# Homes for two loaded weight tiles of a Strassen product: the hi and lo rings instead of buffers of v and x

## The chip, the core and the metric

The kernel runs on one core of a Trainium2 chip. The metric is the device time of one execution in microseconds (us); smaller is better. A second number, the span, is the time from the first to the last instruction of a profiled execution.

## What is computed

Two layers of a decoder trunk on 256 tokens of width 1024, all in float32. Each layer is a half-step feed-forward block (FFN), a mixer, and a second FFN, each with a residual and a layer norm:

```python
def _swiglu(x, w1, w3, w2):
    return (jax.nn.silu(x @ w1) * (x @ w3)) @ w2
...
    for l in range(DEPTH):
        h = _swiglu(x, ffn_w1[l, 0], ffn_w3[l, 0], ffn_w2[l, 0])
        x = _layernorm(ALPHA * x + 0.5 * h, ln_g[l, 0], ln_b[l, 0])
        h = _mixer(x, l, w_in[l], ...)
        x = _layernorm(ALPHA * x + h, ln_g[l, 1], ln_b[l, 1])
        h = _swiglu(x, ffn_w1[l, 1], ffn_w3[l, 1], ffn_w2[l, 1])
        x = _layernorm(ALPHA * x + 0.5 * h, ln_g[l, 2], ln_b[l, 2])
```

`w1` and `w3` are 1024 x 2816, `w2` is 2816 x 1024. There are so four FFNs and four multiplications by `w2`. They are called stage one to four here, in the order in which they run. The mixer plays no part in what follows.

## The kernel before

**Split multiplication.** A float32 matrix is multiplied as the sum of a rounded part (hi) and the rest (lo): ACT copies the weights to the rounded type (hi), DVE subtracts hi from the weights (lo), and PE makes three matmuls for each piece: hi by hi, lo by hi, hi by lo. Every weight that is used goes this way: SP loads 1 MB (128 x 2048) into a buffer of the `raw` pool (`fetch`, line 159), then `stream` (176) or `pieces` (359) splits it in two halves of 128 x 1024, each into one buffer of the `hi` pool (`whi` in the profile) and one of the `lo` pool (`wlo`). `raw` has 4 buffers, `hi` and `lo` have 8 each (line 46); a hi or lo buffer holds 4 KB a partition and is free again when PE has read it.

**The FFN.** In the order of PE, which is written out by hand: products by `w1` and `w3` in column blocks, with one more block done by Strassen's scheme in between (`seven`, line 837: seven block products in place of eight; sums of weight blocks are made on DVE). Then the last `w13a` columns (`gemm_a2`, 285): four halves of hi are multiplied in one pass (line 295, L295 in the profile), then their four halves of lo in a second pass (L302). So w13a holds four lo buffers into the second pass. The next stretch is `w2`.

**The w2 stage** (`gemm_seven`, 377). The first eight row blocks of `w2` (1024 rows, 1024 columns) are split in four blocks w11, w12, w21, w22 of 1 MB each and multiplied by Strassen's scheme; each product is 12 matmuls (`product`, 369; L373). Between the products, one unit (`between`, 412; L402, 12 matmuls) of the remaining rows is done, from chunks of 1 MB that `rest` streams in (two units a chunk). The program's order is:

- load w11 as r1 and split it (p1); load w12 as **r2**; r1 += r2 (`plus`, 353, on DVE, L356)
- product p1; unit; load and split w21, product; add w22 to r2 with accumulating DMAs on POOL's queue (`gather`, 347); load w22 as **r3**
- unit; split r1 (now w11 + w12), product, `fold` the result into the residual (line 602, L605 `xtok` in the profile)
- unit; split r3, product; unit; r1 += r3, split, product, fold; add w21 to r1 with accumulating DMAs
- unit; split r2, product, fold; two units; split r1, product, fold; then the second column half of the remaining rows

r2 and r3 are the two tiles that are loaded to be summed up. **Before**, their homes are called `spare` (lines 924 and 925): r2's halves lie in the two `val` buffers of the `act` pool, which in the mixer hold the values v of the attention and in the FFN the `planes` tiles of blocks n = 0 and n = 2; r3 lies in one buffer of the `xs` pool, whose two buffers hold the split x that w1 and w3 are multiplied by, until the L302 pass has read it. The same scheme in the w13 block (`seven`, lines 859 and 864) has its r2 and r3 in two buffers of `hi` and two of `lo`.

**What sets the order.** PE's order is the program's. On ACT and DVE the splits and the `plus` of the FFN from its second column block on are chained in the program's order (`inline`, 150, and `behind`, 155); other instructions are put between them. SP's, POOL's and the rest of ACT's and DVE's order is made when the program is built, by the framework: the instruction with the lowest number of `step` (109) that has its inputs and a buffer goes first, and a buffer goes to whoever asks for it once it is free. On the chip each queue then runs strictly in that order and waits on semaphores.

Of the kernel before, what the change touches and what calls it, by code (L numbers as in the profile page):

```python
# [11 lines left out]
F32 = mybir.dt.float32  # L12
# [8 lines left out]
P = 128  # L21
D = 1024
# [15 lines left out]
HC = CH // 2  # L38
# [16 lines left out]
def trunk(ctx, tc, x, xT, w13a, w13b, w2, wb, wqk, wu, wg, wgr, wbr, wbrr, wo, gateb, gatebr, sgug, sgub, sguwT, sgubias, lam, diffg,  # L55
# [7 lines left out]
    hi_pool = ctx.enter_context(tc.tile_pool(name="hi", bufs=HL))  # L63
    lo_pool = ctx.enter_context(tc.tile_pool(name="lo", bufs=HL))
    xs = ctx.enter_context(tc.tile_pool(name="xs", bufs=2))
    act = ctx.enter_context(tc.tile_pool(name="act", bufs=26))
# [7 lines left out]
    def name(s):  # L74
        serial[0] += 1
        return f"{s}_{serial[0]}"
# [32 lines left out]
    def step():  # L109
        chunk[0] += 1  # L110
        tc.cur_priority = chunk[0] * STEP
# [43 lines left out]
    def behind(ins):  # L155

        return tc.issue_after(ins) if ins is not None else nullcontext()

    def fetch(src, width=CH, raw=None):

        step()
        if raw is None:
            raw = raw_pool.tile([P, CH], F32, tag="raw", name=name("raw"))
        for g in gate:
            g[0] -= 1
        while len(gate) > 1 and gate[1][0] < 0:
            gate.pop(0)
        with behind(gate[0][1] if gate and gate[0][0] < 0 else None):
            if isinstance(raw, list):
                for j, v in enumerate(raw):  # L170
                    loaded[0] = nc.sync.dma_start(v, src[:, j * HC : (j + 1) * HC]).ins
            else:
                loaded[0] = nc.sync.dma_start(raw[:, :width], src).ins
        return raw
# [149 lines left out]
    def gemm_b(src, kts, xh, xl, done, tail=4, last=()):  # L324
# [13 lines left out]
        for t in range(NT):  # L338
            for ps, o, n in blocks[t]:
                for k, piece in held:  # L340
                    rows_b(ps, t, k, piece, xh, xl, kts, o, n)
                done(t, ps[:, :n], o, n)

    def halved(v):
        return v if isinstance(v, list) else [v[:, o : o + HC] for o in range(0, CH, HC)]

# [6 lines left out]
    def plus(raw, more):  # L353
        for v, m in zip(halved(raw), halved(more)):
            with behind(line[1]):
                inline(V, V.tensor_tensor(out=v, in0=v, in1=m, op=ALU.add).ins)  # L356
        return raw
# [16 lines left out]
                          skip_group_check=True)  # L374
            beat(0.25)

    def gemm_seven(src, xh, xl, sums, spare, ln, done):

# [31 lines left out]
        def between():  # L412
            k, piece = next(first)
            for t in range(NT):
                rows(t, 0, k, piece)

        r1 = fetch(w11)
        p1 = pieces(r1)
        r2 = fetch(w12, raw=spare[0])
        plus(r1, r2)  # L420
        product(bx, a11, p1, True, False)
        ln.fold(0, 0, bx, ALU.add, True)
        between()
        product(q[0][0], a12, pieces(fetch(w21)), False, False)
        gather(r2, w22)
        r3 = fetch(w22, raw=spare[1])
        between()
        product(bz, sums[0], pieces(r1), True, False)
        ln.fold(1, 1, bz, ALU.add, True)
# [313 lines left out]
    def ffn(l, f, i, norm, last=False):  # L743
        xh, xl = parts(both)
# [11 lines left out]
        hh, hl = hv(h_hi), hv(h_lo)  # L756
# [42 lines left out]
        held, sums = {}, []  # L799
# [37 lines left out]
        def seven(src, x_sums):  # L837
# [18 lines left out]
            yield  # L856
            if norm:
                crossed(fetch(w21))
            r2 = fetch(w12, raw=[hi_pool.tile([P, HC], F32, tag="hi", name=name("r2")) for _ in range(2)])
            if norm:  # L860
                yield
            product(bz, x_sums[0], pieces(plus(r1, r2)), True, False)
            A.activation(v1, bz, AF.Copy)
            r3 = fetch(w22, raw=[lo_pool.tile([P, HC], F32, tag="lo", name=name("r3")) for _ in range(2)])
            yield
            product(bx, x_sums[1], pieces(plus(r1, r3)), False, False)
            A.activation(v0, bx, AF.Copy)
# [50 lines left out]
        for j in range(FA, FT - 4, 2):  # L918
            for m, z in gemm_a2([w13a[l, f, j - FA + m] for m in range(2)], both, lambda m: t512("silu")):
# [1 line left out]
                silu[0] = A.activation(s, s, AF.Silu).ins  # L921
                V.tensor_tensor(out=s, in0=s, in1=z[:, T:], op=ALU.mult)
                split(*(v[-1][:, (j - FA + m) * T : (j - FA + m + 1) * T] for v in (h_hi, h_lo)), s)
        spare = [[act.tile([P, D], F32, tag="val", name=name("spare"), bufs=2) for _ in range(2)],
                 xs.tile([P, 4, 512], F32, tag="x", name=name("spare")).rearrange("p k c -> p (k c)")]
        ln = Norm(l, i, 2.0 * ALPHA, 4.0 * EPS, s[:, :1], last)

        def done(t, p, c, n):
# [1 line left out]
            if c + n == D:  # L930
                ln.finish(t, 1.9)

        gemm_seven([w2[l, f, c] for c in range(2)], hh, hl, sums, spare, ln, done)
        return ln.close()

    def mixer(l, i, norm):
# [388 lines left out]
```

## Time and profile before

| what | value |
|---|---|
| median of 3 runs | 1200.97 us (1199.14 to 1205.47) |
| profiled execution | 1208.93 us |
| its span | 1206.9 us |
| mean granted TensorE clock | 0.997 |
| HBM read | 249.10 MB, 207 GB/s over the span |
| the chain that ended last | PE 87%, DMA 5%, DVE 5% |
| of it, loads into `spare` (r2, r3) | 3.5% |

A row of a timeline is: start in us, duration in us, engine, line of the kernel, operation, tile written <- tiles read, shapes, count (xN: N instructions of one kind merged), and in brackets the idle time of the engine ahead of it and what ended that. SPq rows are DMAs that SP issues; their duration is that of the issue, not of the transfer. A row of the waits view is: who waited for whom, us in all, times, longest. A row of windows is: the window, its length, then for PE, PEld, DVE, ACT and POOL the busy time and the count of instructions, then the granted clock, the share of the DMA engines and GB/s. A row of a tile view is: line, engine, operation, tiles, count, then the least, median and greatest duration in ns and the first and last start in us. A row of DMA issues ends with the size of one and the median us from issue to landing. Buffer numbers are left out of names: `spare` is r2 and r3 of the w2 stages, `raw<-in_w` are loads of w2.

### The profile page before, as it was taken

The page shows a single profiled execution, that of the slowest core. Times are in us where ns is not written, and L with a number is a line of the kernel's source. Part 1 is how long each engine was busy: PE and PEld are TensorE (multiplying, and loading weights), DVE is VectorE, ACT ScalarE, POOL GpSimd, SP SyncE. Part 2 cuts the span into 40 slices and gives each one's busy share as a digit, 9 for nine tenths or more (in the row PEclk, how much of TensorE's full clock was granted, in tenths as well). Part 3 has the DMA queues.
Part 4 walks back from the last instruction along what each step waited for, and adds up shares of the span by engine and source line. Part 5 has one row for each costly group of instructions (what it writes and reads, how often), then busy time and mean ns, then how long its engine had stood idle before and what let it go on. Part 6 is the DMA issues. An engine that isn't in the chain of part 4 may idle for free.

```text
span 1206.9 us, 16650 instructions
## 1 busy us (share of the span) xinstructions
PE 1186.2 (98%) x5771; PEld 995.5 (82%) x5771; DVE 1012.0 (84%) x1558; ACT 824.1 (68%) x1418; POOL 296.6 (25%) x356
## 2 busy tenths in 40 slices
PE   9999899999999999999999999999999999999898
PEld 7888688888888888887888888788888888888777
DVE  6889878877778989879899878988966989989685
ACT  6688557559964676885567875676788556679650
POOL 1111301137520210071020070004564012103400
PEclk9999999999999999999999999999999999999999
DMA  9869784767855758697768698586675764886870
GB/s 348 282 194 280 241 292 169 254 201 216 263 190 189 242 175 272 195 284 219 268 206 266 179 277 275 202 288 227 217 211 192 250 192 153 281 257 221 210 241 36
DMA packets 129220, 276.14 MB, mean 229 GB/s; under 512 B 89024, under 2 KB 90096, under 8 KB 104560
## 3 DMA queue, kind: packets, MB, share of 16 engines
q1 hardware_dynamic: 121392, 248.80, 61.6%
q0 software_dynamic: 7312, 25.76, 9.2%
q8 instruction: 45, 0.74, 0.2%
q10 hardware_dynamic: 432, 0.52, 0.2%
q14 instruction: 39, 0.32, 0.1%
HBM read 249.10 MB, written 1.05 MB: 207 GB/s over the span
## 4 chain that ended last, share of the span: by engine, by line
PE 87%; DMA 5%; DVE 5%; ACT 1%; issue 1%; SPq 0%; ACTq 0%; DVEq 0%
PE bank L283 45%; PE bank L295 13%; PE sbank L373 9%; PE bank L302 7%; PE bank L402 5%; DMA spare<-in_w 3%; PE sbank L402 3%; PE bank L512 2%; DVE wlo L249 1%; DMA raw<-in_w 1%; DVE wlo L197 1%; PE sbank L984 1%; DVE raw L356 1%; PE sbank L1040 1%; PE sbank L1158 1%
## 5 line engine op out<-in xcount | busy, mean ns | idle before, releaser
L197 DVE TENSOR_TENSOR wlo<-raw,whi 128x1024 fp32r<-128x1024 f32 (+1 forms) x374 | 414.0, 1134 | 50.1 <-ACT whi L195 35.1
L195 ACT ACTIVATE whi<-raw 128x1024 fp32r<-128x1024 f32 (+1 forms) x378 | 351.5, 958 | 119.2 <-PE bank L283 43.8
L283 PE MATMUL bank<-whi,x 128*128 128x512 f32 x1224 | 386.5, 390 | 0.0
L283 PEld LDWEIGHTS bank<-whi,x 128*128 128x128 f32 x1224 | 229.9, 188 | 47.3
L283 PE MATMUL bank<-wlo,x 128*128 128x512 f32 x612 | 238.5, 390 | 0.0
L295 PE MATMUL bank<-x,whi 128*128 128x512 f32 x640 | 153.3, 392 | 0.0
L295 PEld LDWEIGHTS bank<-x,whi 128*128 128x128 f32 x640 | 118.3, 188 | 23.7
L247 ACT ACTIVATE whi<-raw 128x1024 fp32r<-128x1024 f32 (+1 forms) x96 | 92.6, 982 | 65.4 <-DVE raw L356 31.2
L283 PEld LDWEIGHTS bank<-wlo,x 128*128 128x128 f32 x612 | 115.0, 188 | 23.4
L249 DVE TENSOR_TENSOR wlo<-raw,whi 128x1024 fp32r<-128x1024 f32 (+1 forms) x96 | 110.7, 1166 | 20.1 <-ACT whi L247 19.8
L229 POOL COPY seven<-seven 128x512 uint16<-128x512 uint16 x16 | 64.7, 4102 | 108.7 <-ACT whi L195 82.1
L302 PEld LDWEIGHTS bank<-x,wlo 128*128 128x128 f32 x640 | 81.4, 192 | 2.9
L302 PE MATMUL bank<-x,wlo 128*128 128x256 f32 x640 | 82.6, 284 | 0.0
L402 PE MATMUL bank<-whi,hhi 128*128 128x512 f32 (+1 forms) x182 | 68.8, 378 | 2.9 <-DVE silu L305 2.9
L402 PE MATMUL bank<-wlo,hhi 128*128 128x512 f32 (+1 forms) x182 | 68.1, 374 | 0.0
L402 PE MATMUL bank<-whi,hlo 128*128 128x512 f32 (+1 forms) x182 | 68.0, 374 | 0.0
L960 POOL TENSOR_TENSOR swap<-swap,sin_t 128x512 f32<-128x512 f32 x16 | 26.4, 1649 | 103.3 <-DVE wlo L197 46.1
L719 POOL COPY nvia<-ntwo 128x256 uint16<-128x256 uint16 x20 | 9.9, 544 | 153.3 <-DMA ntwo<-nvia 109.0
L303 ACT ACTIVATE r<-bank 128x256 f32<-128x256 f32 x96 | 33.9, 371 | 13.1 <-PE bank L302 13.0
L402 PEld LDWEIGHTS bank<-whi,hhi 128*128 128x128 f32 x182 | 34.4, 189 | 9.7 <-DVE silu L305 3.8
L373 PE MATMUL sbank<-whi,sum 128*128 128x512 f32 x96 | 33.9, 416 | 8.4 <-DVE xtok L605 8.4
L373 PE MATMUL sbank<-whi,xhs 128*128 128x512 f32 x128 | 42.0, 390 | 0.0
(286 smaller groups left out, 2164.7 us busy)
## 6 DMA issues: line engine op xcount, KB each, us to landing
raw<-in_w13b SPq DMA_DIRECT2D x68, 1024.0 KB, 5.4
raw<-in_w SPq DMA_DIRECT2D x32, 1024.0 KB, 7.1
raw<-in_wb SPq DMA_DIRECT2D x16, 1024.0 KB, 5.3
raw<-in_wqk SPq DMA_DIRECT2D x16, 1024.0 KB, 6.3
r<-in_w13b SPq DMA_DIRECT2D x16, 512.0 KB, 5.9
raw<-in_w13a SPq DMA_DIRECT2D x8, 1024.0 KB, 4.8
raw<-in_wgr SPq DMA_DIRECT2D x8, 1024.0 KB, 5.2
raw<-in_wg SPq DMA_DIRECT2D x8, 1024.0 KB, 5.4
```

The lines of the kernel that those rows point to most:

```text
L195: inline(A, A.activation(h, r, AF.Copy).ins)
L197: low = eng.tensor_tensor(out=w, in0=r, in1=h.bitcast(F32), op=ALU.subtract).ins
L229: eng.tensor_copy(out=o, in_=i)
L247: a = A.activation(hi, src, AF.Copy).ins
L249: return a, eng.tensor_tensor(out=lo, in0=src, in1=hi.bitcast(F32), op=ALU.subtract).ins
L283: PE.matmul(ps, xx, w, start=start and n == 0, stop=stop and n == 2)
L295: PE.matmul(b[-1], hi[:, k * P : (k + 1) * P], xc(k), start=k == 0, stop=False)
L302: PE.matmul(b[n][:, :T], lo[:, k * P : (k + 1) * P], xc(k)[:, :T], start=False, stop=k == KT - 1)
L303: emptied[0] = A.activation(r[:, s], b[n][:, T:], AF.Copy, scale=scale).ins
L373: PE.matmul(ps, x[o](k), y, start=start and k == n == 0, stop=stop and k == 3 and n == 2, skip_group_check=True)
L402: PE.matmul(q[c][t][:, :n] if o == 0 else more[:, :n], x(k, t), y, start=k == 8 and m == 0 and (c, t) != (1, 0), stop=k == FT - 1 and m == ...
L960: turned_by[0] = G.tensor_tensor(out=s3, in0=s3, in1=s, op=ALU.mult).ins
```

## The change

`gemm_seven` no longer gets `spare`. r2 lies in two buffers of the `hi` pool and r3 in two of the `lo` pool, asked for at the place of their loads; r3 is so loaded by two DMAs of 512 KB instead of one of 1 MB. The new helper `homes` makes such a pair; the w13 block uses it too, for the same buffers as before.

```diff
+    def homes(pool, tag):
+        return [pool.tile([P, HC], F32, tag=tag, name=name("home")) for _ in range(2)]
+
...
-    def gemm_seven(src, xh, xl, sums, spare, ln, done):
+    def gemm_seven(src, xh, xl, sums, ln, done):
...
         r1 = fetch(w11)
         p1 = pieces(r1)
-        r2 = fetch(w12, raw=spare[0])
+        r2 = fetch(w12, raw=homes(hi_pool, "hi"))
         plus(r1, r2)
         product(bx, a11, p1, True, False)
         ln.fold(0, 0, bx, ALU.add, True)
         between()
         product(q[0][0], a12, pieces(fetch(w21)), False, False)
         gather(r2, w22)
-        r3 = fetch(w22, raw=spare[1])
+        r3 = fetch(w22, raw=homes(lo_pool, "lo"))
...
-            r2 = fetch(w12, raw=[hi_pool.tile([P, HC], F32, tag="hi", name=name("r2")) for _ in range(2)])
+            r2 = fetch(w12, raw=homes(hi_pool, "hi"))
...
-            r3 = fetch(w22, raw=[lo_pool.tile([P, HC], F32, tag="lo", name=name("r3")) for _ in range(2)])
+            r3 = fetch(w22, raw=homes(lo_pool, "lo"))
...
-        spare = [[act.tile([P, D], F32, tag="val", name=name("spare"), bufs=2) for _ in range(2)],
-                 xs.tile([P, 4, 512], F32, tag="x", name=name("spare")).rearrange("p k c -> p (k c)")]
...
-        gemm_seven([w2[l, f, c] for c in range(2)], hh, hl, sums, spare, ln, done)
+        gemm_seven([w2[l, f, c] for c in range(2)], hh, hl, sums, ln, done)
```

## The prediction

> **What bounds the kernel now.** First the page: how full the engines are.
>
> ```profile
> span 1206.9 us, 16650 instructions
> PE 1186.2 (98%) x5771; PEld 995.5 (82%) x5771; DVE 1012.0 (84%) x1558; ACT 824.1 (68%) x1418; POOL 296.6 (25%) x356
> ```
>
> PE is busy nearly all the time, and the change gives it no instruction more or less. So it can only touch what PE loses: its waits, and time at a lower clock. PE's waits over the whole span, from the waits view:
>
> ```profile
> PE sbank L373 <- DVE xtok L605: 9.0, 4, 5.4
> PE bank L402 <- DVE silu L305: 2.9, 2, 2.5
> PE bank L373 <- DVE bc L571: 1.5, 1, 1.5
> ```
>
> L373 and L402 are the products of the Strassen stages; these rows all fall into the four w2 stages. (The view's three other rows are the kernel's start and end.) Together they are 9.0 + 2.9 + 1.5 = 13.4 us. The same view by windows over stages two, three and four:
>
> ```profile
> PE sbank L373 <- DVE xtok L605: 1.7, 1, 1.7
> PE bank L402 <- DVE silu L305: 0.4, 1, 0.4
> ...
> PE sbank L373 <- DVE xtok L605: 0.6, 1, 0.6
> ...
> PE sbank L373 <- DVE xtok L605: 1.3, 1, 1.3
> ```
>
> So stage one has 5.4; stage two 1.7 and 0.4; stage three 0.6; stage four 1.3, the 1.5 and the other 2.5 of the silu row. The longest one also costs clock; here the window after it, and one over stage four's 2.5 us wait:
>
> ```profile
> 146.00:153.00 7.00, 6.15 (x15) 4.88 (x16) 6.95 (x8) 6.12 (x7) 1.76 (x2) 0.51 0.44 102
> ...
> 1135.00:1156.00 21.00, 16.98 (x76) 13.44 (x74) 19.09 (x28) 11.72 (x20) 1.94 (x3) 1.00 0.74 242
> ```
>
> The column after POOL's is the granted clock: 0.51 for 7 us after the 5.4 us wait, 1.00 through stage four. The dip costs about 7.0 x 0.49 = 3.4 us. All that the w2 stages lose is so 13.4 + 3.4 = **16.8 us**, the ceiling of any gain.
>
> Who is late? Stage one, by timelines of SP, PE, ACT and DVE:
>
> ```profile
> 124.66 0.33 SPq L173 DMA_DIRECT2D spare<-in_w  x1
> ...
> 113.86 7.42 PE L295 MATMUL bank<-x,whi 128*128 128x512 f32 x32
> 121.11 4.00 PE L302 MATMUL bank<-x,wlo 128*128 128x256 f32 x32
> 146.85 0.77 PE L373 MATMUL sbank<-whi,sum 128*128 128x512 f32 x1 [5.40 <-DVE xtok L605]
> ...
> 138.02 1.06 ACT L247 ACTIVATE whi<-spare 128x1024 fp32r<-128x1024 f32 x1 [4.55 <-DMA spare<-in_w]
> ...
> 139.63 0.69 DVE L249 TENSOR_TENSOR hlo<-planes,hhi 128x512 fp32r<-128x512 f32 x1 [4.12 <-ACT hhi L247]
> 142.38 2.35 DVE L249 TENSOR_TENSOR wlo<-spare,whi 128x1024 fp32r<-128x1024 f32 x2
> 144.89 1.22 DVE L356 TENSOR_TENSOR raw<-raw,spare 128x1024 f32<-128x1024 f32 x1
> 146.03 0.68 DVE L605 SCALAR_TENSOR_TENSOR xtok<-xtok,sbank 128x512 f32<-128x512 f32 x1
> ```
>
> r3 (the second spare, one 1 MB load) lies in a buffer of x, and x is read until PE is nearly through the L302 pass: SP issues it at 124.66. It is there at 138.0. ACT, which works in order, stands 4.55 us before it with the hhi split queued behind; DVE stands 4.12 us; the fold that PE waits for is at the end of that queue. The other stages, by DVE's and SP's timelines:
>
> ```profile
> 544.35 1.23 DVE L356 TENSOR_TENSOR raw<-raw,spare 128x1024 f32<-128x1024 f32 x1 [7.19 <-DMA spare<-in_w]
> ...
> 720.06 1.23 DVE L356 TENSOR_TENSOR raw<-raw,spare 128x1024 f32<-128x1024 f32 x1 [5.20 <-DMA spare<-in_w]
> ...
> 1136.79 1.23 DVE L356 TENSOR_TENSOR raw<-raw,spare 128x1024 f32<-128x1024 f32 x1 [8.50 <-DMA spare<-in_w]
> 1137.93 1.22 DVE L197 TENSOR_TENSOR wlo<-raw,whi 128x1024 fp32r<-128x1024 f32 x1
> ...
> 1110.34 2.56 SPq L173 DMA_DIRECT2D raw<-in_w  x2
> ...
> 1118.57 0.38 SPq L171 DMA_DIRECT2D spare<-in_w  x1
> 1124.11 4.83 SPq L220 DMA_TRANSPOSE planes<-planes  x2
> 1128.99 0.57 SPq L171 DMA_DIRECT2D spare<-in_w  x1
> ```
>
> Here it is the second half of r2: its val buffer comes free late, and SP has two transposes before it (the one half is issued at 1118.57, the other at 1128.99). The sum of r1 and r2 stands in the written chain of DVE, so all later splits stand behind it, 5 to 8.5 us.
>
> **The change part by part.** No matmul, split, sum or byte is added. r2 takes two of the eight hi buffers from its load to its split, r3 two of the eight lo buffers until it is split and added; r3 becomes two loads of 512 KB.
>
> *When r2 can start.* In stage four w11 and the first rest chunk are issued from 1110.34 on; r2 stands between them in the program. It needs two hi buffers. Those of the last w13 product and of the last two w13 streams come free one after another before the L295 pass (which in stage one begins at 113.86); w13a holds four until its quarters of that pass end. So both halves of r2 start at best before the L295 pass, about ten us ahead of 1128.99, and at worst in the middle of it. *r3* follows w21 on SP and takes the two lo buffers that the last streams leave, about ten us before its 124.66; at worst it waits for the L302 pass, as now.
>
> *What is pushed back.* With r3 in the lo ring, the splits of the first rest chunk and of w21 must wait for w13a's four lo buffers, which come free in quarters of the L302 pass (stage one: 122.1, 123.1, 124.1, 125.1). Their price, and the DVE times that they replace:
>
> ```profile
> L356 DVE TENSOR_TENSOR raw<-raw,spare x16: 1212/1218/1724, 117.3 to 1155.9; 128x1024 f32<-128x1024 f32 x16
> L247 ACT ACTIVATE whi<-spare x16: 1041/1044/1062, 138.0 to 1161.0; 128x1024 fp32r<-128x1024 f32 x16
> L249 DVE TENSOR_TENSOR wlo<-spare,whi x16: 1215/1218/1225, 142.4 to 1162.9; 128x1024 fp32r<-128x1024 f32 x16
> ...
> 120.04 2.86 DVE L197 TENSOR_TENSOR wlo<-raw,whi 128x1024 fp32r<-128x1024 f32 x2
> ```
>
> Stage one: the chunk's first lo goes from 120.04 to 122.1, four splits of 1.22 us end near 127 instead of 126.2, and PE reads the last of them after 130. Covered by some 3 us; nothing. Stages two to four: DVE took the chunk up only after its stall (1137.93); now it can at the first quarter of the L302 pass, that is, by the row below, at 1132.4: **5.5 us earlier**.
>
> ```profile
> 1131.42 4.00 PE L302 MATMUL bank<-x,wlo 128*128 128x256 f32 x32
> ...
> 163.52 5.44 PE bank L402 x24
> ```
>
>  If the cover went, it would be up to four splits, 4.9 us a stage.
>
> *What goes.* Stage one: ACT no longer stands before r3, so DVE's queue runs 4.12 us earlier and the fold ends at 142.6. PE's wait falls from 5.4 to about 1.3; with the 2.1 us of the chunk's delay handed on it would be 3.4. I take 1.5 (the first is nearer, DVE has time to catch up): 3.9 us go. A wait of 2.5 us left the clock at 1.00 in stage four, so the 3.4 us of the dip go too: 7.3. Stage two: the fold's 1.7 and 0.4 before it, both under what DVE gains: 2.1. Stage three: 0.6. Stage four: 2.5 + 1.5 against 5.5 us gained: 4.0; its 1.3 comes much later, behind the gathered r1, and stays. Sum 14.0. Against it I set 0.5 us a stage, 2.0, for what comes up next: stage three, where DVE stalled least, still has 0.6. **Net 12.0 us.**
>
> *DMA.* r3 now shares the stretch of the other loads:
>
> ```profile
> 1118.00:1135.00 17.00, 17.00 (x90) 14.66 (x90) 8.23 (x10) 11.01 (x15) 9.78 (x8) 1.00 1.10 260
> ```
>
> The DMA share (the number before the last) is full there already, 1.10. 1 MB at 260 GB/s delays what follows by 4.0 us. That is the second rest chunk and the transposes of planes; the chunk is read by PE several units later (a unit is 12 matmuls, by the L402 row above 2.72 us), the transposed rows later still. Covered; without cover at most 4.0 us a stage, 16 in all, which with nothing gained would be 1217.
>
> The loads by size, stage one:
>
> ```profile
> spare<-in_w SPq DMA_DIRECT2D x2, 512.0 KB, 4.9
> spare<-in_w SPq DMA_DIRECT2D x1, 1024.0 KB, 13.3
> ```
>
> Two halves one behind the other would take 9.8 us, r3 took 13.3 in the crowd. A rule of the Trainium skill speaks against the halves (DMA: Bandwidth & Descriptors, section "Measured (HBM→SBUF, 128 partitions, SWDGE, issued from GpSimd)"): loads should be of 1 MiB or more to get three quarters of the peak. By it r3 would land later for the same start; the trace agrees in part, 4.9 us for 512 KB, though the 13.3 us of the 1 MB load is longer than two of these. As r3 starts ten us earlier, the sum by the one or the other is the same.
>
> The profiled execution took 1208.9 us with a span of 1206.9; the median of the runs is 1201.0. 1208.9 - 12.0 = 1196.9, and on the median **1189 us**.
>
> **The rivals.**
>
> *Too late to matter (the change does not do what it says).* The buffers are handed out while instructions are put in order; if ACT's and DVE's splits get them first, r2 starts in the L295 pass and r3 in the L302 pass, about when they do now. Then only r2's second half gains, 0 to 4 us: 1197 to 1201, taken 1199. Against it: SP stands idle before these loads, and asks first.
>
> *Starved rings (slower).* From r2's load to its split six hi buffers serve, and six lo for r3. If a buffer is freed less than 1.04 + 1.22 = 2.26 us before PE needs its refill, PE stands 2.26 us. Five products lie in that stretch: 11.3 us a stage, 45 in all. By count six halves are the running product and two units ahead, so 2 x 2.72 = 5.4 us of lead, and that decides: the rival holds once ACT or DVE come to a freed buffer over 3.1 us late. If half the refills are late it costs 22.6 and the 14.0 are still gained: 1209.6, from 1203 up to 1224. Against it stands the same use of the pools in the w13 products:
>
> ```profile
> L171 SPq DMA_DIRECT2D r<-in_w13b x16: 327/382/702, 39.3 to 1058.7; - x16
>   DMA r<-in_w13b: 3.6, 2
> ...
>   DMA spare<-in_w: 39.0, 8
> ```
>
> (r is the page's short name for r2 and r3 there.) Engines stood before those loads 3.6 us in 2 cases, before the spares 39.0 us in 8, and PE has no wait there. For it: there half the pieces are read for both row blocks, here units follow faster. The Trainium skill gives this rival its rule (Perfetto Trace Analysis, section "Optimization Strategy"): the same gap again and again on the engine that should be full can mean too few buffers for the next tile. By the rows of before the gaps have another cause, late loads; after it, equal gaps at each product would be that rule.
>
> **How the numbers follow.** Forecast 0.60, with its own range 1184 (all 16.8 us) to 1195; too late 0.18; starved 0.22. About 0.5%, 6 us, is what a measurement of this kernel can tell from no change. Forecast is faster, too late within it, starved slower: 0.60, 0.18, 0.22. The range 1183 to 1210 leaves out the worse half of the last.
>
> **What would show it.** DVE's idle rows before L356 (7.19, 5.20, 8.50) should vanish or fall under 4, ACT's row at r3 (4.55) vanish, the clock hold 1.00 at 146 to 153, PE's waits fall from 13.4 to under 4. SP should issue r3 before the L302 pass. It would be wrong if r3 is still issued at its end, if PE waits at L373 or L402 for splits (whi, wlo) instead of the fold, or if waits come up before the w2 stages, in w13a.

## The result, and the profile after

After takes 1198.39 us (median of 14 runs, 1196.38 to 1202.18), before in the same comparison 1202.41 us (14 runs, 1199.14 to 1207.47): ratio 0.9963, 95% interval [0.9947, 0.9979], so 4.0 us faster. Two more comparisons, on two different chips, gave after 0.9922 [0.9899, 0.9945] and 0.9951 [0.993, 0.9973] of before. The sign was forecast, the size (12 us, to 1189) was not: by the medians the gain is a third to two thirds of that.

The profiled execution took 1199.19 us, against 1208.93 before. The first lines of its page:

```profile
span 1197.5 us, 16664 instructions
PE 1182.9 (99%) x5771; PEld 992.8 (83%) x5771; DVE 1011.9 (85%) x1558; ACT 825.8 (69%) x1418; POOL 285.5 (24%) x356
```

PE has the same 5771 matmuls. Its waits at the lines of the products and units (L373 is now L376, L402 is L405, L605 is L608):

```profile
PE sbank L376 <- DVE xtok L608: 4.0, 4, 1.9
...
PE bank L376 <- DVE wlo L249: 1.7, 1, 1.7
PE bank L376 <- DVE bc L574: 1.2, 2, 1.0
```

4.0 + 1.7 + 1.2 = 6.9 us in place of 13.4. The stretch behind the third product of stage one, by windows (the number behind POOL's is the granted clock):

```profile
146.00:153.00 7.00, 7.00 (x33) 5.79 (x32) 6.92 (x7) 6.86 (x7) 1.77 (x2) 1.00 0.47 94
```

33 matmuls at full clock where before had 15 at 0.51.

**Where r2 and r3 start.** SP's and DVE's timelines of stage one; `home` is now r2 (the first two) and r3 (the third). PE's first product begins at 124.7. The first line is before's r2, the others are after's:

```profile
107.65 4.83 SPq L171 DMA_DIRECT2D spare<-in_w  x2
...
117.60 0.56 SPq L171 DMA_DIRECT2D home<-in_w  x1
118.28 1.25 SPq L220 DMA_TRANSPOSE planes<-planes  x1
119.62 0.54 SPq L171 DMA_DIRECT2D home<-in_w  x1
120.22 9.36 SPq L173 DMA_DIRECT2D raw<-in_w  x2
129.67 0.54 SPq L171 DMA_DIRECT2D home<-in_w  x1
...
122.38 1.23 DVE L359 TENSOR_TENSOR raw<-raw,home 128x1024 f32<-128x1024 f32 x1 [5.29 <-DMA home<-in_w]
125.03 1.23 DVE L359 TENSOR_TENSOR raw<-raw,home 128x1024 f32<-128x1024 f32 x1 [1.42 <-DMA home<-in_w]
```

Here both loads start **later** than before: r3 at 129.67 (before 124.66), r2 at 117.6 and 119.6 (before from 107.65 on), so late that DVE now stands 5.29 + 1.42 us, where before it stood not at all; the 1.7 and 1.0 us at w21's product are the price. What r3 waits for, SP's waits from 104 to 135 show:

```profile
SPq L173 <- DVE wlo L197: 10.4, 2, 8.5
```

The 8.5 us are the time from 120.7 to 129.25, in which SP stands before a load of w2 into `raw`, until DVE has split the first rest chunk (L197). That split stands behind the two late sums. r3 is issued right behind this load, 5 us after PE went on from the L302 pass to the first product. By then PE had read w13a's lo buffers, so that here SP's order, and no longer the L302 pass, holds r3. In stage four SP stands 8.1 us in the same place (first product at 1129.4; before at 1135.2):

```profile
1117.19 0.33 SPq L171 DMA_DIRECT2D home<-in_w  x1
1118.31 3.71 SPq L220 DMA_TRANSPOSE planes<-planes  x2
1122.11 0.53 SPq L171 DMA_DIRECT2D home<-in_w  x1
...
1131.18 0.99 SPq L171 DMA_DIRECT2D home<-in_w  x2
...
1122.31 1.23 DVE L359 TENSOR_TENSOR raw<-raw,home 128x1024 f32<-128x1024 f32 x1 [1.85 <-DMA home<-in_w]
1125.94 2.15 DVE L359 TENSOR_TENSOR raw<-raw,home 128x1024 f32<-128x1024 f32 x1 [2.41 <-DMA home<-in_w]
```

r2's second half is issued 7.3 us ahead of the product (before 6.2), and DVE stands 1.85 + 2.41 us before the two halves instead of 0.81 + 8.50; r3 still starts 1.7 us behind the product's start.

**What changed in stage one.** ACT's and DVE's timelines:

```profile
133.46 0.62 ACT L247 ACTIVATE hhi<-planes 128x512 fp32r<-128x512 f32 x1
133.98 1.99 ACT L195 ACTIVATE whi<-raw 128x1024 fp32r<-128x1024 f32 x2
139.46 2.27 ACT L247 ACTIVATE whi<-home 128x1024 fp32r<-128x1024 f32 x2 [3.49 <-DMA home<-in_w]
...
135.34 0.68 DVE L249 TENSOR_TENSOR hlo<-planes,hhi 128x512 fp32r<-128x512 f32 x1
...
141.49 1.22 DVE L249 TENSOR_TENSOR wlo<-home,whi 128x1024 fp32r<-128x1024 f32 x1
142.62 0.68 DVE L608 SCALAR_TENSOR_TENSOR xtok<-xtok,sbank 128x512 f32<-128x512 f32 x1
```

ACT still stands 3.49 us before r3. But the last hhi split (133.46) is now **ahead** of r3's split; before, it was queued behind it (138.02, then 138.99). The last five hhi splits are now ahead of the two splits of a rest chunk as well (L195, 133.98); before, they were queued behind the first of these (129.50). And the fold stands on DVE behind one lo split of r3, where before it was behind two and one half of the sum. The rows are the same instructions in another order: with other buffers for the loads, the framework wrote ACT's and DVE's queues anew.

### The profile page after: what moved, and what is told of

It reads as the page before. It is cut to its first block, busy times and chain, and to the rows that moved or that the text cites. A ratio compares the mean times of both kernels' runs of the same rounds, so it can differ in the third digit from the quotient of the medians.

```text
span 1197.5 us, 16664 instructions
## 1 busy us (share of the span) xinstructions
PE 1182.9 (99%) x5771; PEld 992.8 (83%) x5771; DVE 1011.9 (85%) x1558; ACT 825.8 (69%) x1418; POOL 285.5 (24%) x356
## 4 chain that ended last, share of the span: by engine, by line
PE 90%; DMA 4%; DVE 3%; issue 2%; ACT 1%; SPq 0%; POOL 0%; DVEq 0%; ACTq 0%; POOLq 0%
PE bank L283 46%; PE bank L295 14%; PE sbank L376 10%; PE bank L302 7%; PE bank L405 6%; PE sbank L405 3%; DMA home<-in_w 2%; PE bank L515 1%; PE sbank L985 1%; DMA raw<-in_w 1%; DVE wlo L197 1%; DMA raw<-in_w13b 1%; DVE wlo L249 1%; PE sbank L1041 1%; PE sbank L1159 1%
## 5 line engine op out<-in xcount | busy, mean ns | idle before, releaser
L197 DVE TENSOR_TENSOR wlo<-raw,whi 128x1024 fp32r<-128x1024 f32 (+1 forms) x374 | 413.4, 1133 | 50.1 <-ACT whi L195 35.3
L195 ACT ACTIVATE whi<-raw 128x1024 fp32r<-128x1024 f32 (+1 forms) x378 | 350.6, 959 | 112.2 <-PE bank L283 43.6
L302 PEld LDWEIGHTS bank<-x,wlo 128*128 128x128 f32 x640 | 81.4, 191 | 2.9
L229 POOL COPY seven<-seven 128x512 uint16<-128x512 uint16 x16 | 55.6, 3523 | 114.9 <-ACT whi L195 54.7
L302 PE MATMUL bank<-x,wlo 128*128 128x256 f32 x640 | 82.6, 283 | 0.0
L405 PE MATMUL bank<-whi,hhi 128*128 128x512 f32 (+1 forms) x182 | 68.3, 375 | 0.1
L405 PE MATMUL bank<-whi,hlo 128*128 128x512 f32 (+1 forms) x182 | 67.9, 373 | 0.0
L405 PE MATMUL bank<-wlo,hhi 128*128 128x512 f32 (+1 forms) x182 | 67.9, 373 | 0.0
L359 DVE TENSOR_TENSOR raw<-raw,home 128x1024 f32<-128x1024 f32 x32 | 41.2, 1293 | 25.4 <-DMA home<-in_w 21.7
L303 ACT ACTIVATE r<-bank 128x256 f32<-128x256 f32 x96 | 34.5, 372 | 15.4 <-PE bank L302 15.3
L376 PE MATMUL sbank<-whi,xhs 128*128 128x512 f32 x128 | 42.0, 389 | 0.0
L247 ACT ACTIVATE whi<-home 128x1024 fp32r<-128x1024 f32 x32 | 33.2, 1052 | 10.4 <-DMA home<-in_w 6.9
```

Of the source, the lines that this page charges most:

```text
L195: inline(A, A.activation(h, r, AF.Copy).ins)
L197: low = eng.tensor_tensor(out=w, in0=r, in1=h.bitcast(F32), op=ALU.subtract).ins
L229: eng.tensor_copy(out=o, in_=i)
L247: a = A.activation(hi, src, AF.Copy).ins
L302: PE.matmul(b[n][:, :T], lo[:, k * P : (k + 1) * P], xc(k)[:, :T], start=False, stop=k == KT - 1)
L303: emptied[0] = A.activation(r[:, s], b[n][:, T:], AF.Copy, scale=scale).ins
```

## The experiments

All kernels were timed in five rounds against before, except one that was profiled once. The experiments came in five sets. The ratio is always to before, timed alongside on the same chip.

**First set: which of the two moves, and how much does before vary?**

*before_again* is before unchanged. 

> The kernel before once more, with a second profile. Theory 'odd execution': the profile on which the sum was made shows stage one at its worst; a second one has PE's wait there under 3 us and no window at half clock, so its w2 waits are about 9 us in all instead of 13.4 plus 3.4, and its span is 4 to 6 us shorter. Rival 'always so': again about 5.4 us in stage one and 0.5 of the clock for 7 us; then 5 us of the gain were really lost elsewhere. Time against before: 0 (within 1 us) by both.

Measured: 1206.62 us, ratio 0.9996 [0.9971, 1.002]; profiled at 1204.12 us. So this chip's before is 4 to 5 us slower than the 1202.41 above. Waits of its w2 stages:

```profile
PE sbank L373 <- DVE xtok L605: 6.8, 6, 4.5
...
PE bank L402 <- DVE bc L571: 0.8, 1, 0.8
...
PE bank L402 <- DVE silu L305: 0.3, 1, 0.3
PE bank L373 <- DVE wlo L249: 0.2, 1, 0.2
```

8.1 us, not the 13.4 on which the prediction was summed: the theory had the total right. Of stage one the rival was nearer: its wait is 4.5 us, not under 3, and the 6.8 us at half clock are there again.

*r2_only*: r2 in hi buffers, r3 still in the buffer of x.

```diff
-        r2 = fetch(w12, raw=spare[0])
+        r2 = fetch(w12, raw=homes(hi_pool, "hi"))
```

> Only r2 moves to the hi ring; r3 stays in the buffer of x. Theory 'r2 carries it': r3 was issued at the end of the L302 pass in both kernels, so its home matters little; this one gives the whole gain, -3 to -5 us, with DVE's stalls before the sum (7.2, 5.2, 8.5) down to 2 to 5. Rival 'r3 carries it': the halves of r3 and its place outside x give the gain; then this one is -1 us or slower, since r2 comes 9 us later in stage one.

Measured: 1200.23 us, 0.994 [0.9915, 0.9965]. Full clock in stage one, 7.2 us of waits.

*r3_only*: the other half.

```diff
-        r3 = fetch(w22, raw=spare[1])
+        r3 = fetch(w22, raw=homes(lo_pool, "lo"))
```

> Only r3 moves to the lo ring; r2 stays in the buffers of v. Theory 'r2 carries it': -1 to +1 us, DVE's stalls before r2 stay at 5 to 8.5 us. Rival 'r3 carries it': -3 to -5 us.

Measured: 1205.49 us, 0.9993 [0.9971, 1.0014]. 9.9 us of waits. The windows of both kernels over stage one's third product, first r2_only:

```profile
143.00:153.00 10.00, 10.00 (x46) 8.29 (x45) 9.93 (x10) 7.08 (x8) 1.76 (x2) 1.00 0.52 98
```

Then r3_only:

```profile
143.00:153.00 10.00, 9.61 (x35) 7.82 (x36) 9.69 (x10) 7.66 (x8) 1.76 (x2) 0.83 0.59 114
```

r2's move alone gives a gain of after's size; r3's alone gives none that can be measured. Whether r3's adds something on top of r2's is a question for the next set.

*fold_before*: before, with the sum of r1 and r3 written into DVE's order behind the fold, in all stages.

```diff
-        ln.fold(1, 1, bz, ALU.add, True)
+        folded = ln.fold(1, 1, bz, ALU.add, True)
...
+        with behind(folded):
+            plus(r1, r3)
-        product(bx, sums[1], pieces(plus(r1, r3)), False, False)
+        product(bx, sums[1], pieces(r1), False, False)
```

> The kernel before with one order changed: DVE's sum of r1 and r3 is queued behind the fold of the product ahead of it, instead of by chance before or after it. Theory 'fold behind the sum': PE's waits at L373 for xtok (5.4, 1.7, 0.6, 1.3) each shrink by about 1.2 us, one sum; -2 to -4 us in all. Rival 'r3's landing': the fold is late because r3's splits are, the order saves nothing; within 1 us.

Measured: 1209.61 us, 1.0013 [0.9988, 1.0038]. Stage one still waits 4.4 us; in the other stages the third product waits no more, but the last one, that of the gathered r1, does in its place: 8.7 us in all, against 8.1 in before_again.

**Second set: who gets which buffer?**

*after_again* is after unchanged. 

> The kernel after once more, as the base that the other three kernels of this call are compared with, on one chip. On the chip of the calls before, the kernel with r2 alone moved stood at 0.994 of before, and after's own comparison gave 0.9963 [0.9947, 0.9979]. Theory "r2 carries it": 0.994 to 0.997 here, no half-clock stretch in stage one, PE waits of the w2 stages 6 to 9 us. Rival "r3's move adds a gain of its own": under 0.993.

Measured: 1200.01 us, 0.9922 [0.9899, 0.9945], 5.5 us of waits, full clock. That is under the rival's 0.993, but r2_only's interval reaches it.

*r2_first*: r2 asked for one line earlier.

```diff
         r1 = fetch(w11)
-        p1 = pieces(r1)
         r2 = fetch(w12, raw=homes(hi_pool, "hi"))
+        p1 = pieces(r1)
```

> After, with r2's two hi buffers asked for in the program before those of the first product's pieces (one line moved up). Theory "the buffers of one tag are handed out in the order of the program": r2 gets the hi buffers that come free first (those that the first product had), and the first product's pieces get r2's. SP then issues r2 in stage one at 105 to 113 us instead of 117.6 and 119.6, DVE's idle time of 5.29 and 1.42 us before the two sums of stage one goes, and with it the 1.7 and 1.0 us that PE stands at w21's product; the first product's pieces are split 3 to 10 us later, which nobody waits for since they were split that much ahead. 2 to 4 us less than after. Rival "a ring of eight is short by two buffers, whoever gets them": the wait moves to the first product, PE stands 3 us or more at its start (124.7 in after), and the time is equal to after's or up to 4 us above.

Measured: 1196.27 us, 0.9896 [0.9873, 0.9919]. The means of this and of after_again, six runs each, differ by 3.1 us (95% interval 0.7 to 5.5, worked out from the runs). SP's and DVE's timelines in stage one:

```profile
107.43 1.69 SPq L171 DMA_DIRECT2D home<-in_w  x2
...
128.96 0.95 SPq L171 DMA_DIRECT2D home<-in_w  x2
...
120.40 2.87 DVE L359 TENSOR_TENSOR raw<-raw,home 128x1024 f32<-128x1024 f32 x2
```

One line in the program moves both halves of r2 from 117.6 and 119.6 to 107.4, and the 5.29 + 1.42 us before the sums are gone. So, as far as these moves show, the buffers of one tag are handed out **in the program's order**; the sentence in the part on the kernel before, that a buffer goes to whoever asks for it once it is free, was wrong, and the prediction built on it. A wait of 2.0 us is new, at the first unit (L405), so that the gain is less than what went.

*r3_early*: after, with r3 asked for right behind r2.

```diff
         r2 = fetch(w12, raw=homes(hi_pool, "hi"))
+        r3 = fetch(w22, raw=homes(lo_pool, "lo"))
...
-        r3 = fetch(w22, raw=homes(lo_pool, "lo"))
```

> After, with r3 asked for right behind r2 (its load one queue place ahead of w21's, and its two lo buffers ahead of those of the first rest chunk). Theory "program order": r3 gets the lo buffers that the last streams leave and is issued 5 to 10 us before the first w2 product, as the prediction wanted it, instead of 1.7 to 5.6 us behind it; no engine stands before r3. In return the first rest chunk's and w21's lo splits wait for the L302 pass. If the prediction's reckoning of that (covered by 3 us or more) holds, the time is 0 to 2 us below after's. Rival "the lo ring is the bound": the first chunk's lo buffers come free only within the L302 pass, DVE stands there and PE waits for wlo at the first rest rows or w21's product, 1 to 2 us a stage, so 3 to 8 us above after.

Measured: 1197.72 us, 0.9906 [0.9883, 0.9929]; its mean is 1.8 us below after_again's (interval -3.7 to +0.1). Stage four on SP:

```profile
1122.09 1.48 SPq L171 DMA_DIRECT2D home<-in_w  x3
```

The three loads of this row are r2's second half and r3. r3 so starts some 4 us before the first product, which begins at 1126.9. PE's waits over the span:

```profile
PE bank L376 <- DVE wlo L249: 2.4, 4, 1.0
PE bank L376 <- DVE bc L574: 2.0, 2, 1.0
...
PE sbank L376 <- DVE xtok L608: 1.0, 2, 0.8
```

The fold's waits fall from 2.4 (after_again) to 1.0 us, but those for wlo and the instruction behind it on DVE (bc) rise from 3.1 to 4.4. Both theories were half right. That the lo splits which now follow r3 in the pool take its place behind the L302 pass would explain it, but was not looked into.

*r2_first_x*: r2_only with the same line moved up.

```diff
-        p1 = pieces(r1)
         r2 = fetch(w12, raw=homes(hi_pool, "hi"))
+        p1 = pieces(r1)
```

> Before, with r2 alone in hi buffers, asked for ahead of the first product's pieces; r3 stays in the buffer of x. Theory "program order": as for the same move in after, so 1 to 3 us less than the 0.994 that r2 alone gave, 0.991 to 0.993; in stage one r2 is issued before 113, and r3 at about the start of the first product. Rival "r3 in x then sets the end": with r2 early again in stage one DVE's queue once more meets r3's late landing, the fold waits as before, PE stands 4 to 5 us at the third product and the clock falls for 7 us: 0.996 to 1.0.

Measured: 1198.24 us, 0.9913 [0.9893, 0.9934]. r3 in x, issued at 127.8 and landed 15.3 us behind the first product's start by ACT's first split of it (before: 13.1), makes the third product of stage one wait under 1 us. So r3's landing alone did not make it wait 5.4 us before. The mean of r2_first, in which r3 is moved too, is 2.1 us below this one's (interval 0.05 to 4.1, worked out from the six runs each): with r2 early, r3's move seems to add a little of its own.

**Third set: a better version, and before once more.**

*r2_first_again*: 

> The kernel with r2 ahead of the first product's pieces once more, as the base of this call. Theory "program order": again 3 to 5 us under after's 1200.0, a ratio of 0.988 to 0.992 to before. Rival "the gain of that kernel was one of the chip's good hours": 0.992 to 0.997.

Measured: 1195.78 us, 0.9918 [0.9895, 0.9941].

*both_early*: r2_first with r3 asked for right behind the first product's pieces (the same move of r3's line as above). 

> r2 ahead of the first product's pieces, and r3 right behind them: both moves together. r3 alone moved up cost waits for wlo at w21's product (0.8 + 1.2 us in stage one, 1.2 + 1.2 in stage four) and took away the 2.4 us of the fold's wait in stage four. Theory "each move saves its own wait": with r2 there 17 us ahead, DVE is free for the late lo splits, the waits for wlo fall under 1 us a stage, and the w2 stages' waits fall from 5.5 us to under 3: 1 to 3 us below r2_first_again. Rival "the lo ring is short by two": DVE still waits for w13a's lo buffers whatever r2 does, the waits for wlo stay at 2 us in stages one and four: equal to r2_first_again within 1 us, or above it.

Measured: 1195.28 us, 0.9912 [0.9887, 0.9936]: the lowest median, but its mean differs from r2_first_again's by only 0.5 us (interval -1.8 to +0.9). Waits 3.8 us, against 4.5. Those for wlo and bc stay at 2.3 us in stage one, as its rival had it; in stage four they are gone.

*r2_first_fold*: r2_first with the fold edit of fold_before. 

> r2 ahead of the first product's pieces, and the sum of r1 and r3 written into DVE's order behind the fold that PE waits for. In before, this left the time as it was (ratio 1.0013): the wait went to the product of the gathered r1. Theory "the fold was late because of DVE's queue, and the queue now has slack": the fold's waits (1.0 us in stage one, 1.5 in stage four) go, none comes up at the last product, 1 to 3 us below r2_first_again. Rival "the gather of r1 is the chain": the sum, and with it r1's gather on POOL's queue, comes later, PE waits 0.9 to 2 us a stage at the last product as it did in before: equal or up to 3 us above.

Measured: 1196.05 us, 0.9917 [0.9894, 0.994], as r2_first_again. Waits fell to 3.3 us, 1.3 of it at the last product of stage four, but 3.4 us ran at half clock in stage one.

*before_look*: before, one profile. 

> The kernel before, one more profile. Two profiles of it so far: 1208.9 us with 13.4 us of PE waits in the w2 stages and 6.9 us at half the clock, and 1204.1 us with about 9 us of waits and 6.8 us at half the clock. Theory "before's time varies with how late the spares land": the waits of the w2 stages plus half of the time at half clock differ from those profiles by about as much as the time does (within 2 us). Rival "before varies elsewhere": the same waits and another time.

Measured: 1204.97 us; 9.2 + 1.2 + 0.2 = 10.6 us of waits, 6.8 us at half clock. Against the first profile 2.8 us less of waits and 4.0 us less time; against the second 2.5 us more waits and 0.9 us more time, with 6.8 us at half clock in all three. So waits and time differ from one another by 1.2 and 1.6 us, within the 2 us expected.

**Fourth and fifth set: what took stage one's wait away?**

*order_before*: before, in stage one alone r3's splits behind the fold.

```diff
-        ln.fold(1, 1, bz, ALU.add, True)
+        folded = ln.fold(1, 1, bz, ALU.add, True)
...
-        product(bz, sums[3], pieces(r3), False, False)
+        stages.append(folded)
+        with behind(folded if len(stages) == 1 else None):
+            p3 = pieces(r3)
+        product(bz, sums[3], p3, False, False)
```

> Before, with r2 and r3 where they were; in stage one alone the splits of r3 are written into ACT's and DVE's order behind the fold that PE waits for (in before the fold stands behind both lo splits of r3 and one half of the sum). Theory "stage one's gain is the fold's place in DVE's order": PE's wait at the third product falls from 4.7 to 6.3 us to 1.5 to 3 us (the first lo split of r3 is then what is late), the half clock goes or falls to 3.4 us, and the time is 3 to 6 us under before: ratio 0.995 to 0.998. Rival "it is r3's landing, whatever the order": the wait only passes to r3's splits, 4 us or more, with the same 6.8 us at half clock; ratio 0.999 to 1.002.

Measured: 1203.95 us, 0.9994 [0.9973, 1.0016]. The wait at stage one's third product falls to 2.0 us for the fold and 0.6 for wlo, the time at half clock to 3.4 us; the gain in time did not come. ACT's timeline shows what is left:

```profile
137.37 1.06 ACT L247 ACTIVATE whi<-spare 128x1024 fp32r<-128x1024 f32 x1 [2.94 <-DMA spare<-in_w]
138.34 0.61 ACT L247 ACTIVATE hhi<-planes 128x512 fp32r<-128x512 f32 x1
```

The hhi split still stands behind r3's.

*order_after*: after, in stage one alone the fold behind r3's two lo splits and the sum.

```diff
...
+            p3 = pieces(r3)
+            plus(r1, r3)
...
+            with behind(summed[0]):
+                ln.fold(1, 1, bz, ALU.add, True)
...
```

(`summed` holds the first half of the sum.)

> After, with r2 and r3 in the rings; in stage one alone the fold is written behind r3's two lo splits and the sum of r1 and r3. Theory "the fold's place in DVE's order": PE waits 3.5 to 6 us at the third product again, the clock is at half for 3.4 to 6.8 us behind it, and the time is 5 to 8 us above after_base. Rival "the loads": with the loads as in after the fold is late by no more than the instructions put ahead of it less the slack, under 2 us of wait, no half clock, and the time is at most 2 us above after_base.

Measured: 1199.01 us, 0.9949 [0.9929, 0.9968]; the third product of stage one waits 0.9 us, at full clock. My theory that the fold's place in DVE's queue was the cause falls.

*after_base* is after unchanged. 

> The kernel after, as the base for order_after. Both theories: 0.992 to 0.997 of before, no half clock in stage one, waits of the w2 stages 5.5 to 7 us.

Measured: 1197.39 us, 0.9951 [0.993, 0.9973], 5.8 us of waits, and 3.4 us at half clock, in stage four. The means of order_after and after_base differ by 1.0 us (interval -0.7 to +2.7).

*both_first*: after, with both loads ahead of the first product's pieces.

```diff
         r1 = fetch(w11)
+        r2 = fetch(w12, raw=homes(hi_pool, "hi"))
+        r3 = fetch(w22, raw=homes(lo_pool, "lo"))
         p1 = pieces(r1)
-        r2 = fetch(w12, raw=homes(hi_pool, "hi"))
...
-        r3 = fetch(w22, raw=homes(lo_pool, "lo"))
```

> After, with both loads, r2 and r3, ahead of the first product's pieces in the program. Theory "program order": r3 too now gets buffers that are free early, both are issued 10 us or more before the first product, and only the lo splits of the first chunks stand behind w13a; 0 to 2 us better than with r3 right behind the first product's pieces (ratio 0.988 to 0.992 to before). Rival "the lo ring": the first product's own lo splits now wait for w13a's lo buffers, PE stands 2 us or more at the first product in each stage, and the time is 3 to 8 us above, at or above after's.

Measured: 1197.42 us, 0.9932 [0.991, 0.9955]; it waits 2.5 us at w21's product and 3.4 us run at half clock. No better than after_base by what these runs can tell.

*hhi_before*: before, in stage one alone r3's splits behind the last hhi split (`last_hhi` holds that instruction; `stages` counts the stages).

```diff
...
-        product(bz, sums[3], pieces(r3), False, False)
+        stages.append(sums)
+        with behind(last_hhi[0] if len(stages) == 1 else None):
+            p3 = pieces(r3)
+        product(bz, sums[3], p3, False, False)
```

> Before, with r2 and r3 where they were; in stage one alone ACT's splits of r3 are written behind the last split of the planes tiles (hhi), so that ACT waits for r3's load with nothing of DVE's queued behind it. Theory "ACT's order": DVE's idle time of 2 to 4 us before the hlo split goes, the fold's wait in stage one falls to 1 to 2.7 us, and the half clock shrinks from 6.8 to 3.4 us or none; 3 to 6 us of the profile's span, ratio 0.995 to 0.999. Rival "the loads": r3's load lands as late as before, and the fold stands behind r3's lo splits, so that the wait stays above 3.5 us with 6.8 us at half clock; ratio 0.999 to 1.001.

Measured: 1203.09 us, 0.997 [0.9951, 0.9989]. ACT's, DVE's and PE's timelines, and then the window:

```profile
131.35 1.14 ACT L247 ACTIVATE hhi<-planes 128x512 fp32r<-128x512 f32 x2
136.54 2.01 ACT L247 ACTIVATE whi<-spare 128x1024 fp32r<-128x1024 f32 x2 [4.05 <-DMA spare<-in_w]
...
140.35 1.22 DVE L356 TENSOR_TENSOR raw<-raw,spare 128x1024 f32<-128x1024 f32 x1
141.49 0.68 DVE L610 SCALAR_TENSOR_TENSOR xtok<-xtok,sbank 128x512 f32<-128x512 f32 x1
...
142.31 0.47 PE L373 MATMUL sbank<-whi,sum 128*128 128x512 f32 x1 [1.67 <-DVE xtok L610]
```

```profile
143.00:153.00 10.00, 10.00 (x46) 8.28 (x45) 9.95 (x10) 6.87 (x8) 1.77 (x2) 1.00 0.69 153
```

The order of the loads, the buffers and the fold's place are those of before. ACT still stands 4.05 us before r3; DVE no longer does, the fold runs at 141.49 instead of 146.03, PE waits 1.67 us instead of 5.40, and the clock stays full. **With ACT's order changed, most of stage one's wait is gone in this profile.** In time the change is worth 0.3% (0.1 to 0.5), less than after's 0.4 to 0.8%.

That r3 is all that ACT's order is about, this does not show. In hhi_before ACT began r3's first split 12.4 us behind the first product's start, in before's three profiles 13.1 to 13.9 us behind it. And r3 is not the only late load ahead of an hhi split. ACT's and DVE's timelines of before_again:

```profile
134.17 1.06 ACT L195 ACTIVATE whi<-raw 128x1024 fp32r<-128x1024 f32 x1 [5.14 <-DMA raw<-in_w]
138.72 1.06 ACT L247 ACTIVATE whi<-spare 128x1024 fp32r<-128x1024 f32 x1 [0.57 <-DMA spare<-in_w]
...
135.57 0.43 DVE L249 TENSOR_TENSOR hlo<-silu,hhi 128x256 fp32r<-128x256 f32 x1 [3.19 <-ACT hhi L247]
140.33 0.69 DVE L249 TENSOR_TENSOR hlo<-planes,hhi 128x512 fp32r<-128x512 f32 x1 [0.15 <-ACT hhi L247]
```

Here ACT stood 5.14 us before a rest chunk and hardly before r3, DVE lost its time at the first hhi split and not at the last, and PE waited 4.55 us all the same. In before_look ACT stood 3.85 us before the chunk, in the first profile 1.87, in hhi_before not at all. After has the last hhi splits ahead of both loads, hhi_before only ahead of r3; no run moved the chunk's splits alone. Nor is the order always enough: in r3_only, too, the hhi splits stand ahead of r3's, ACT did not stand before the chunk, and 2.4 us of the fold's wait and 3.4 us of half clock were left. How the rest of after's gain divides between the chunk's splits, r2's earlier second half and the fold's place stays open.

*hhi_fold_before*: both places changed (r3's splits behind the fold too). 

> Before, with both places changed in stage one: r3's splits behind the last hhi split on ACT, and behind the fold on DVE. Theory "the order of ACT and DVE together": the wait at the third product falls to 0.6 to 1.5 us and no half clock is left, as in the kernels with r2 in the ring, with both loads where they were in before; ratio 0.993 to 0.998. Rival "the loads": what is late is r3 itself, PE then waits 2.5 us or more for r3's hi or lo split at that product and 3.4 us stay at half clock; ratio 0.998 to 1.001.

Measured: 1202.59 us, 0.9981 [0.9965, 0.9998]. The third product waits 0.3 and 0.6 us, but the last product of stage one now waits 2.3 us, with 3.4 us at half clock behind it.

**The balance.** From each profile: its span, less all that the waits view lists for PE, less half of the time at half clock. What remains is nearly the same 1187 us in all 20 profiles (1186.6 to 1189.5, 17 of them up to 1187.9). Waits by stage are from the waits view by windows:

| kernel | profiled us | stage one | two | three | four | at half clock | other waits | rest |
|---|---|---|---|---|---|---|---|---|
| before | 1208.9 | 5.4 | 2.1 | 0.6 | 5.3 | 6.8 | 3.2 | 1186.9 |
| before_again | 1204.1 | 5.6 | 0.8 | 1.2 | 0.5 | 6.8 | 3.2 | 1187.4 |
| before_look | 1205.0 | 6.1 | 1.4 | 2.9 | 0.2 | 6.8 | 1.9 | 1187.1 |
| after | 1199.2 | 3.2 | 0.9 | 0.8 | 2.1 | 0 | 3.6 | 1187.0 |
| after_again | 1198.0 | 2.7 | 0 | 0.2 | 2.5 | 0 | 2.7 | 1188.1 |
| after_base | 1200.9 | 2.0 | 0.5 | 0.4 | 2.8 | 3.4 | 4.9 | 1186.8 |
| hhi_before | 1197.0 | 1.7 | 0.5 | 2.7 | 0.4 | 0 | 2.7 | 1187.2 |

The balance closes: hardly any of the time lies outside PE's waits and its clock. In the three pairs (the second and third pair two chips each) the steady gain is stage one, 8.8 to 9.5 us of waits and clock before, 2.0 to 3.2 after. Stages two and three give about 2 us. Stage four gives nothing against the two later profiles of before; it gets 2 us worse, and in after_base another 1.7 for the 3.4 us at half clock there.

## Why the prediction was wrong, step by step

**The base, the step that failed.** "1208.9 - 12.0 = 1196.9, and on the median 1189." The sum was made on an execution that lost 16.8 us in the w2 stages, and subtracted from a median 8 us below it, as if those 8 us came from elsewhere. They came from the same waits: before's other profiles lost 11.5 and 14.0, and by the balance in the section above (1187 us, 2 to 3 us of other waits, 2 us around the span) an execution of 1201 us loses some 9 to 10. On its own base the sum stands nearly: 1196.9 was forecast for the profile, 1199.2, 1198.0 and 1200.9 were measured. The prediction's own lines could have shown it: with all 16.8 us gone, the profiled execution would take 1192.1, so that neither 1189 nor the low end of 1183 was within reach. The base of 1201.0 was itself low: it is the median of 3 runs, and those of the later comparisons, of 11 to 31 runs each, were 1202.4 to 1208.0.

**Stage one, 7.3 us: nearly right in size, wrong in reason.** 8.8 less 3.2 is 5.6 us in the first pair, 6.3 and 7.5 in the others. For that one execution the chain was read rightly (ACT stands before r3 with an hhi split queued behind it, DVE waits for that, the fold is at the end), and in hhi_before, which breaks it at its first link, the wait falls to 1.67 us. In before_again another late load, the rest chunk, stood at its head. But I let r3 come early to break it. r3 came 5 us later, and the wait went with a written order that had changed. A change of buffers was treated as if all queues kept their order. That the half clock would go with the wait was luck in part: the prediction took it from one wait of 2.5 us that left the clock full, and in the runs here waits of 2.0 to 2.9 us brought half clock in 8 of 15 cases (last section).

**r2 and r3 "ten us ahead": wrong.** Buffers of a tag go out in the program's order, and SP's loads go out in SP's. In after r3 was issued 5 us (stage one) and 1.7 us (stage four) behind the first product's start, each time right behind a load for which SP had stood 8.5 and 8.1 us; "at worst it waits for the L302 pass" was too good. r2 in stage one comes behind the first product's hi buffers, which cost 2.7 us that the prediction did not have. r2_first takes those 2.7 us away, and in r3_early r3 starts ahead of the first product. Only r2's second half in stages two and four gained (2 to 5 us in landing against the first profile).

**Stage four, 4.0 us: one execution's loss.** 5.3 us of waits in the first profile, 0.5 and 0.2 in the next two; 2.1 to 2.8 in after. Why the fold there waits about 2 us in after was not settled; in r3_early it falls to under 1 us, and waits for wlo come up in its place.

**Stages two and three, 2.7 us:** 1.0 us in the first pair, about 2 on the mean of the three. The **allowance** of 2.0 for what comes up next was taken up by stage one's 2.7 at w21's product.

**The rivals.** "Starved rings" did not come: nothing waits at each product. "Too late to matter" had the time (1197 to 1201) and r3's part; but its gain was to come from r2's second half alone, and by the balance it came mostly in stage one, where r2 was later than before. **DMA shared:** covered, as forecast, as far as the waits show: no row of PE's waits in after names a rest chunk's split (L197) or the transposed rows.

**What would show it.** The clock at 146 to 153 is 1.00: as forecast. PE's waits are 6.9, not under 4. DVE's idle rows of 5 to 8.5 us shrank to 2.8 and less, but now there is one before each half of r2: 5.5, 5.2 and 4.3 us in stages two, three and four, against 7.2, 5.2 and 9.3 before, and 6.7 came up in stage one. ACT's row at r3 stayed (4.55, now 3.49). SP issues r3 behind the start of the first product; the prediction had named that as what would prove it wrong.

## What to carry to other kernels

Subtract a sum only from the execution in which its terms were read, and hold the result against that execution with all of its losses gone; when the median lies far below the profile, the terms are too large for it. An in-order engine that stands before a late load costs what is queued behind it: with one independent instruction moved ahead of the load's consumer, the wait that the new buffers were to remove fell from 5.4 to 1.7 us in one profile, and the kernel was 0.3% faster. Look at several profiles before naming the load: here it was not the same one each time. When tiles join a pool that is handed out in program order, the place of the request decides who waits: one line moved up (r2_first) was worth another 3 us, and that kernel, with or without r3 moved up as well, is among the fastest of all that ran.

## What the runs showed of the hardware

The clock did not follow the length of a wait alone. The same wait of 2.0 us at the same instruction (L405, stage one) left the clock full in r2_first and brought half clock in r2_first_x; the windows behind it, r2_first ahead of r2_first_x:

```profile
129.00:134.00 5.00, 3.96 (x17) 3.27 (x18) 4.99 (x12) 3.23 (x8) 0.00 (x0) 1.00 1.05 244
```

```profile
129.00:133.00 4.00, 4.00 (x11) 3.13 (x12) 3.99 (x11) 3.25 (x8) 0.00 (x0) 0.57 1.03 251
```

0.57 over 4 us are 4 x 0.43 x 2 = 3.4 us at half clock. Such stretches lasted 3.4 or 6.8 us in every profile that had one. In the w2 stages waits up to 1.9 us never brought one, those of 2.0 to 2.9 us in 8 of 15 cases, those of 4.4 us and more always. The Trainium skill (TensorE: Matmul & The Clock Gate, section "What's actually happening") has the clock set by the activity in free-running windows of some 3.4 us, and half rate after an idle one. The lengths agree, and that chance decides between equal waits fits free-running windows; but waits of 2.0 to 2.9 us, shorter than such a window, sufficed here, and the measurement decides.
